# Mixture-of-experts stage: six second tiles of 64 places, with the high and the low parts of the tokens side by side in the stationary operand

## The chip, the cores and the metric

The kernel runs on one core of one Trainium2 chip. The metric is the device time of one execution in microseconds, as the median of several runs. The engines are called PE (TensorE; PEld are its weight loads), ACT (ScalarE), DVE (VectorE), POOL (GpSimd) and SP (SyncE, which issues transfers).

## The reference, cut to what matters

One layer of a hybrid model on 1024 tokens of width 1024: projections, sparse attention and a state-space mixer, an output projection, a layer norm, then a mixture of 16 experts with two experts per token, and a last layer norm. The change touches the experts alone:

```python
gates = ...            # top 2 of 4 experts in the best of 4 groups, times the group's probability
y = jnp.zeros_like(h)
for e in range(N_EXPERTS):                                  # 16
    hid = jax.nn.silu(h @ w_gate[e]) * (h @ w_up[e])        # 1024 -> 256
    y = y + gates[..., e:e + 1] * (hid @ w_down[e])         # 256 -> 1024
x = layer_norm(ALPHA * x + y, ln2_g, ln2_b)
```

All of it is fp32. The kernel keeps fp32's precision by splitting each operand of a product into a high part, which is its value in the reduced type that PE multiplies, and a low part, the remainder.

## The kernel before, in words

The stages up to the first layer norm are the same in both kernels. The router sorts the tokens into one list per expert (`lst`, 1152 places each, empty ones filled with indices that the indirect transfers skip). `order()` ranks the experts by how many tokens they have; ranks 0 to 3 are picked early, from the first blocks of tokens. An expert is worked on in tiles of 128 places of its list. `plan()` (L99) says which tiles are written out: ranks 0 and 1 have their first tile early, while the last two token blocks are still mixed, and their second tile in the main loop; ranks 2 to 7 have two tiles; ranks 8 to 15 have one. The order of the experts is `TURN` (L96): 0, 1, 2, 3, 8, 9, 4, 10, 11, 5, 12, 13, 6, 14, 15, 7. What an expert has over its written-out places (`CAPS`, L38: 256 places for ranks 0 to 7, 128 for the others) goes through a loop under `tc.If` at the end (L1282 ff.), which is skipped if no expert has more.

`expert_tile` (L892) does one tile:

1. `gather` (L885) fetches the tile's 128 rows of the normed tokens by an indirect transfer that POOL issues (`xg`).
2. PE transposes them in eight pieces (L898, tile `pt`), ACT casts each half to its high part `th` (helper `hi_act`, L123), DVE subtracts for the low part `tl` (helper `lo_dve`, L126).
3. PE multiplies with the gate and up weights (L909, tile `ag`, 512 columns: 256 of gate, 256 of up): eight pieces of the width, three products each (high by high, low by high, high by low), 24 matmuls.
4. ACT does SiLU on the gate half (L914), DVE multiplies by the up half (L915, `sg`).
5. PE transposes the 256 columns in two pieces (L918, `ph`), ACT and DVE split them again (`hh`, `hl`).
6. PE multiplies with the down weights (L934, tile `ad`, two halves of 512 columns, two pieces, three products: 12 matmuls). DVE multiplies the first half by the gate (L939), ACT the second (L937), into `yt`.
7. POOL issues the indirect scatter-add of `yt` into `yd` (L941).

The weights of an expert come in three pieces: gate and up for the first half of the width (key 0), for the second half (key 1), and down (key d), 1 MB each. `fetch` (L855) issues the transfers from SP into one of `NR` = 5 raw buffers `er`, in turn. `split_expert` (L867) makes the high part on ACT and the low part on DVE, in four quarters, into slots; 12 slots, in the tiles `eb`, `woh` and `wol`, hold two experts, so that an expert's piece goes where that of the expert two turns earlier was. When a piece is split, `more` issues the fetch that will reuse its raw buffer, five pieces further on. `yt` has three buffers, `xg` four, the others two; the gathers run three tiles ahead.

The order of instructions on each engine isn't written by hand: the program is given to a scheduler with a timeline of its own, which fixes for every engine one queue in which nothing overtakes. An instruction that waits in it holds up all that stand behind.

The main loop over the tiles begins at about 618 us of the profile; the scatter-add of the last tile is issued at 844.85.

Of the kernel before, what the change touches and what calls it, by code (L numbers as in the profile page):

```python
# [22 lines left out]
P = 128  # L23
# [13 lines left out]
SL = S + P  # L37
CAPS = ((0, 8, 256), (8, 16, 128))  # L38
XB = 4
# [59 lines left out]
def plan():  # L99
    return [(a, t) for a in TURN for t in ((P,) if a < NEARLY else (0, P) if a < 8 else (0,))]  # L100


# [7 lines left out]
def body(ctx, tc, I, out, dbg):  # L110
# [773 lines left out]

    def gather(ids, al):  # L885
        xg = al([P, D], F32, "xg")
        marks["gather"] = G.indirect_dma_start(out=xg, out_offset=None, in_=hd,
                                               in_offset=bass.IndirectOffsetOnAxis(ap=ids[:, 0:1], axis=0),
                                               bounds_check=S - 1, oob_is_err=False)
        return xg  # L890

    def expert_tile(W, ids, xg, al):  # L892
# [34 lines left out]
        for hf in range(2):  # L927
# [10 lines left out]
            else:  # L938
                V.tensor_scalar(yt[:, fs], ad_, gate, None, op0=OP.mult)  # L939
        yield  # L940
        st_ = G.indirect_dma_start(out=yd, out_offset=bass.IndirectOffsetOnAxis(ap=ids[:, 0:1], axis=0),  # L941
                                   in_=yt, in_offset=None, compute_op=OP.add,
                                   bounds_check=S - 1, oob_is_err=False)
        if "y" in W:
            tc.declare_no_dep(st_.ins, W["y"], reason="the two tiles of one expert hold distinct tokens")
        W["y"] = st_.ins
        yield

    with ExitStack() as ph:
# [253 lines left out]
        with (tc.manual_schedule(engines={getattr(mybir.EngineType, e) for e in MAN}) if MAN else ExitStack()):  # L1203
# [12 lines left out]
            for j in range(NG0):  # L1216
                ids = rp.tile([P, 2], I32, name="ids", bufs=XB + 2)
                SY.dma_start(ids, lst[bass.ds(EE[PLAN[j][0]] * SL + PLAN[j][1], P), :])
                early_q.append((ids, gather(ids, al0), PLAN[j][0]))
            with tc.issue_after(marks["gather"].ins) if NG0 else ExitStack():  # L1220
# [27 lines left out]
    def ids_for(r, t0):  # L1248
        ids = wk.tile([P, 2], I32, name="idt", bufs=len(PLAN) - NG0)
        SY.dma_start(ids, lst[bass.ds(rank(r) * SL + t0, P), :])  # L1250
        return ids, r

# [9 lines left out]
    for i in range(-AHEAD, len(PLAN)):  # L1262
        sp = []
        if NG0 <= i + AHEAD < len(PLAN):
            ids, r = lists.pop(0)
            q.append((ids, gather(ids, al1), r))
        if i >= 0:
# [6 lines left out]
        if i >= 0:  # L1274
            ids, xg, r = q.pop(0)
            t_ = expert_tile(WS[r], ids, xg, al1)
            emit((6, up(t_, HP)), *sp)
# [87 lines left out]
```

## Time and profile before

| | us |
|---|---|
| three runs, median | 889.72 |
| three runs, lowest and highest | 881.93, 892.22 |
| the profiled execution | 886.67 |
| its span | 885.0 |
| PE busy in the span | 784.3 (89%) |
| DVE, ACT, POOL busy | 655.7, 510.3, 240.1 |

The profile is that of one execution. The span goes from the first to the last instruction; the profiled execution's own time is 1.67 us longer. A matmul's end is modelled and overlaps the next one's start, so that the mean of single matmuls is longer than the step from one to the next; the chain of waits goes from start to start. A wait is put down to the releaser that came last.

### The profile page before, as it was taken

The numbers are of one execution on the slowest core, as the hardware profiler recorded it, in microseconds if no ns is written. First come the engines' busy times: TensorE is split into PE (matmuls) and PEld (weight loads), VectorE is DVE, ScalarE is ACT, GpSimd is POOL, SyncE is SP. The second block draws the span as 40 slices with busy tenths as digits, with TensorE's granted clock in tenths as the row PEclk, the third lists the DMA queues.
The fourth block names the chain that finished last, engine by engine and source line by source line (L and its number), as shares of the span: only waits on it lengthen the run. The fifth ranks groups of instructions, "written<-read, shape, count | busy, mean of one in ns | idle before, by whom it ended". The sixth has DMA issues, their size and how long they took to land. (4 is left out here: it accounts for less than half of the span.)

```text
span 885.0 us, 12823 instructions
## 1 busy us (share of the span) xinstructions
PE 784.3 (89%) x4084; PEld 647.0 (73%) x4085; DVE 655.7 (74%) x1619; ACT 510.3 (58%) x1083; POOL 240.1 (27%) x219
## 2 busy tenths in 40 slices
PE   6999789999997899899999999897899899999910
PEld 4798568887775678778888887775688688888700
DVE  3578988869578899778687676686586778887336
ACT  3467777892356677575464332263566767876333
POOL 3211000000377545170100111122433234332236
PEclk9999899999997999999999999899799999999965
DMA  8303122311335313884433323795699898987174
GB/s 245 102 26 96 38 71 81 116 55 60 110 113 186 117 60 111 279 281 163 119 120 120 113 103 120 258 371 156 148 345 316 238 307 270 325 269 231 26 214 192
DMA packets 90598, 147.57 MB, mean 167 GB/s; under 512 B 16645, under 2 KB 62869, under 8 KB 90522
## 3 DMA queue, kind: packets, MB, share of 16 engines
q1 hardware_dynamic: 83098, 129.87, 43.3%
q0 software_dynamic: 7424, 16.81, 8.2%
q8 instruction: 33, 0.54, 0.3%
q14 instruction: 43, 0.35, 0.1%
HBM read 109.78 MB, written 45.25 MB: 175 GB/s over the span
## 5 line engine op out<-in xcount | busy, mean ns | idle before, releaser
L231 PE MATMUL acc<-whl,xh 128*128 128x512 f32 (+1 forms) x384 | 121.4, 390 | 3.9 <-DVE rt L251 2.0
L231 PEld LDWEIGHTS acc<-whl,xh 128*128 128x128 f32 x384 | 72.5, 190 | 19.3 <-ACT whl L123 2.4
L252 POOL TENSOR_TENSOR r<-rt,rt 128x448 f32<-128x448 f32 (+1 forms) x16 | 22.9, 1429 | 196.4 <-DVE rt L251 179.8
L123 ACT ACTIVATE ph<-pt 128x512 fp32r<-128x512 f32 (+1 forms) x80 | 43.3, 551 | 56.4 <-PE pt L776 53.6
L231 PE MATMUL acc<-whl,xl 128*128 128x512 f32 (+1 forms) x192 | 75.7, 395 | 0.0
L909 PE MATMUL ag<-eb,th 128*128 128x512 f32 x192 | 68.7, 422 | 3.7 <-ACT th L123 3.7
L359 PE MATMUL acc<-xh,whl 128*128 128x512 f32 x192 | 64.0, 411 | 6.7 <-ACT u L123 6.7
L941 POOL DMA_INDIRECT yd<-yt,idt x21 | 40.4, 1922 | 103.7 <-ACT hh L123 31.8
L764 ACT ACTIVATE lt<-lt,mn 128x1024 f32<-128x1024 f32 (+7 forms) x64 | 49.3, 773 | 11.2 <-DVE mn L761 10.9
L126 DVE TENSOR_TENSOR plo<-pt,ph 128x512 fp32r<-128x512 f32 (+1 forms) x80 | 49.8, 630 | 6.4 <-ACT ph L123 5.9
L397 ACT ACTIVATE scra<-sc,mid 128x1024 bf16<-128x1024 f32 (+3 forms) x56 | 49.2, 879 | 4.2 <-DVE gef L427 1.7
L359 PEld LDWEIGHTS acc<-xh,whl 128*128 128x128 f32 x192 | 37.8, 199 | 15.4 <-ACT u L123 7.5
L1098 POOL DMA_INDIRECT lst<-pay,idx x16 | 18.3, 1146 | 113.3 <-DVE pay L1095 29.2
L123 ACT ACTIVATE eb<-er 128x512 fp32r<-128x512 f32 x64 | 38.1, 628 | 16.9 <-DMA er<-w_up 10.6
L879 DVE TENSOR_TENSOR eb<-er,eb 128x512 fp32r<-128x512 f32 x64 | 41.6, 687 | 8.2 <-ACT eb L123 4.7
L909 PEld LDWEIGHTS ag<-eb,th 128*128 128x128 f32 x192 | 38.4, 200 | 12.6 <-ACT th L123 4.5
L879 DVE TENSOR_TENSOR woh<-er,woh 128x512 fp32r<-128x512 f32 x64 | 41.7, 686 | 6.2 <-ACT woh L123 2.3
L879 DVE TENSOR_TENSOR wol<-er,wol 128x512 fp32r<-128x512 f32 x64 | 40.8, 683 | 7.2 <-ACT wol L123 4.3
L126 DVE TENSOR_TENSOR tl<-pt,th 128x512 fp32r<-128x512 f32 x48 | 32.3, 685 | 18.3 <-ACT th L123 18.2
L776 PE MATMUL pt<-ident,lt 128*128 128x128 f32 x288 | 44.7, 275 | 1.3 <-ACT lt L764 0.7
L123 ACT ACTIVATE woh<-er 128x512 fp32r<-128x512 f32 x64 | 37.9, 626 | 13.0 <-PE ac L1010 6.7
L1010 PE MATMUL ac<-woh,ai 128*128 128x512 f32 x128 | 43.7, 425 | 0.3 <-DVE xb L1014 0.3
(360 smaller groups left out, 2347.2 us busy)
## 6 DMA issues: line engine op xcount, KB each, us to landing
er<-w_gate SPq DMA_DIRECT2D x32, 512.0 KB
er<-w_up SPq DMA_DIRECT2D x32, 512.0 KB
er<-w_down SPq DMA_DIRECT2D x16, 1024.0 KB
xb<-x SPq DMA_DIRECT2D x16, 512.0 KB
raw<-w_in SPq DMA_DIRECT2D x8, 512.0 KB
qd<-qs SPq DMA_DIRECT2D x8, 512.0 KB
sd<-so SPq DMA_DIRECT2D x8, 512.0 KB
qb<-qd SPq DMA_DIRECT2D x8, 512.0 KB
```

The source lines that it names most:

```text
L123: A.activation(hi, src, AF.Copy)
L126: V.tensor_tensor(lo, src, f(hi), op=OP.subtract)
L231: T.matmul(acc[:, :n], l[:, b, k, :], r[:, k % 2, :n], start=i == 0, stop=i == 3 * KC - 1)
L252: G.tensor_tensor(dst, t1, t2, op=OP.add)
L359: T.matmul(acc, w[:, k, :], xx[:, 4 * hf:4 * hf + 4, k, :], start=i == 0, stop=i == 3 * KC - 1)
L397: A.activation(scra[:, :nk], sc[b], AF.Sign, bias=at, scale=-1.0, accum_out=dst)
L764: A.activation(lt[:, :nk], lt[:, :nk], AF.Exp, bias=mn[:, h:h + 1], scale=-1.0, accum_out=rs[:, h:h + 1])
L776: T.transpose(pt[:, c:c + P], L[b, 2 * p + j][:, kt * P:(kt + 1) * P], ident)
L879: e.tensor_tensor(lo[x], raw[x], f(hi[x]), op=OP.subtract)
L909: T.matmul(ag, l[:, k, :], r[:, k % 4, :], start=i == 0, stop=i == 3 * KC - 1)
L941: st_ = G.indirect_dma_start(out=yd, out_offset=bass.IndirectOffsetOnAxis(ap=ids[:, 0:1], axis=0), in_=yt, in_offset=None, compute_op=OP.a ...
L1010: T.matmul(ac, src[:, o + k % 4, :], w[:, k, fs], start=i == 0, stop=i == 3 * KC - 1)
```

## The change

`plan()` stays; a new function names the second tiles of ranks 2 to 7 as half tiles of 64 places (`HR`), and `CAPS` gives these ranks 192 places in all. For a half tile `half_tile` takes the place of `expert_tile`. Its operand `th` holds for each piece of the width 64 columns of high parts and then 64 columns of low parts of the same tokens. Each piece is multiplied with the high and then with the low part of the weights: two matmuls of 128x512 where there were three. Rows 0 to 63 of the result belong to the high parts, rows 64 to 127 to the low parts; ACT copies the lower rows over, DVE adds them to the upper ones. This is done for gate and up (into `yt`, which serves as the place for that sum too) and for both halves of the down product. The token's gate is multiplied in with the up part, behind the SiLU. The gather and the scatter-add name 64 places. The diff's core:

```diff
-CAPS = ((0, 8, 256), (8, 16, 128))
+CAPS = ((0, 2, 256), (2, 8, 192), (8, 16, 128))
+HR = P // 2
...
+def half(a, t):
+    return a >= NEARLY and t > 0
...
+    def half_tile(W, ids, xg, al):
+        th = al([P, KC, 2, HR], F32R, "th")
+        pt = psum([P, KC, HR], "pt", "pt")
+        for k in range(KC):
+            T.transpose(pt[:, k, :], xg[:HR, k * P:(k + 1) * P], ident[:HR, :HR])
+        hi_act(th[:, :, 0, :], pt)
+        lo_dve(th[:, :, 1, :], pt, th[:, :, 0, :])
+        yield
+        ag = psum([P, 512], "ag", "lg")
+        for k in range(KC):
+            for j, w in enumerate(W[k // 4]):
+                T.matmul(ag, th[:, k], w[:, k % 4, :], start=k + j == 0, stop=k + j == KC)
+            if k % 4 == 3:
+                yield
+        yt = al([P, D], F32, "yt")
+        sg = al([P, 256], F32, "sg")
+        A.activation(yt[:HR, :512], ag[HR:], AF.Copy)
+        V.tensor_tensor(yt[:HR, :512], ag[:HR], yt[:HR, :512], op=OP.add)
+        A.activation(sg[:HR], yt[:HR, :256], AF.Silu)
+        V.scalar_tensor_tensor(sg[:HR], yt[:HR, 256:512], f(ids[:HR, 1:2]), sg[:HR], op0=OP.mult, op1=OP.mult)
+        ph2 = psum([P, 2, HR], "ph2", "po")
+        for k in range(2):
+            T.transpose(ph2[:, k, :], sg[:HR, k * P:(k + 1) * P], ident[:HR, :HR])
+        hh = al([P, 2, 2, HR], F32R, "hh")
+        hi_act(hh[:, :, 0, :], ph2)
+        lo_dve(hh[:, :, 1, :], ph2, hh[:, :, 0, :])
+        yield
+        for hf in range(2):
+            fs = slice(hf * 512, (hf + 1) * 512)
+            ad_ = psum([P, 512], "ad", "sb" if hf else "sa")
+            for k in range(2):
+                for j, w in enumerate(W["d"]):
+                    T.matmul(ad_, hh[:, k], w[:, k, fs], start=k + j == 0, stop=k + j == 2)
+            A.activation(yt[:HR, fs], ad_[HR:], AF.Copy)
+            V.tensor_tensor(yt[:HR, fs], ad_[:HR], yt[:HR, fs], op=OP.add)
+        yield
+        add_rows(W, ids, yt, HR)
+        yield
...
-            t_ = expert_tile(WS[r], ids, xg, al1)
+            ids, xg, r, h = q.pop(0)
+            t_ = (half_tile if h else expert_tile)(WS[r], ids, xg, al1)
```

`gather` and `add_rows` (the scatter-add of `expert_tile`, now a function) take the number of places as an argument. Up to the expert stage the order of instructions is the same but for one more constant. In the stage the scheduler lays out everything anew. Two places:

The first place is on PE, from the end of rank 4's last down matmuls (`ad` of `woh`) on. Before, the rest of rank 10's gate-and-up matmuls follows (`ag` of `wol`), then transposes and matmuls of rank 11 (`ag` of `eb`); rank 12's use of its second gate-and-up piece comes 125 matmuls and 40 transposes after that end:

```order
L934 MATMUL ad<-woh,hl 128x512
L934 MATMUL ad<-woh,hh 128x512
L909 MATMUL ag<-wol,tl 128x512
L909 MATMUL ag<-wol,th 128x512 x2
...
L898 MATMUL pt<-ident,xg 128x128 x4
L909 MATMUL ag<-eb_6648,th 128x512
L909 MATMUL ag<-eb_6648,tl 128x512
```

Now (L989 and L968 are the half tile's down and gate-and-up matmuls, L947 and L922 those of whole tiles) the last three of rank 5's first tile follow, rank 5's half tile, and rank 10's down matmuls (`ad` of `wol`); behind these stand the transposes `ph` of rank 11 and the first twelve matmuls of rank 12:

```order
L989 MATMUL ad<-woh,hh 128x512 x8
L931 MATMUL ph_8334<-ident,sg 128x128 x2
L922 MATMUL ag<-wol,th 128x512
L922 MATMUL ag<-wol,tl 128x512
...
L968 MATMUL ag<-woh,th 128x512 x8
L968 MATMUL ag<-wol,th 128x512 x8
L911 MATMUL pt<-ident,xg 128x128 x4
L947 MATMUL ad<-wol,hh 128x512 x2
```

Down matmuls now stand further behind the gate-and-up matmuls of their tile, so that rank 12's second piece (`ag` of `eb_6651`) is used 43 matmuls and 13 transposes after rank 4's end.

The second place is on ACT, at the end of the stage. Before, the last instructions are those of rank 7's two tiles (the numbered `ph` are the transposed results, `yt` the evictions):

```order
L937 ACTIVATE yt<-ad,idt 128x512
L123 ACTIVATE hh<-ph_9308 128x256
L937 ACTIVATE yt<-ad,idt 128x512
L914 ACTIVATE sg<-ag 128x256
L123 ACTIVATE hh<-ph_9379 128x256
L937 ACTIVATE yt<-ad,idt 128x512
```

Now the copy of the half tile's gate-and-up result into `yt` (L973) stands behind the casts of rank 7's first tile (`ph_9244`), and its SiLU (L975) behind that tile's eviction:

```order
L950 ACTIVATE yt<-ad,idt 128x512
L128 ACTIVATE hh<-ph_9173 128x256
L950 ACTIVATE yt<-ad,idt 128x512
L128 ACTIVATE hh<-ph_9244 128x256
L973 ACTIVATE yt<-ag 64x512
L950 ACTIVATE yt<-ad,idt 128x512
L975 ACTIVATE sg<-yt 64x256
L128 ACTIVATE hh<-ph_9306 128x2x64
L990 ACTIVATE yt<-ad 64x512 x2
```

The half tile's gate-and-up matmuls themselves have moved forward, ahead of rank 14's down matmuls; the copy waits for the scatter-add of rank 14, whose `yt` buffer it takes.

## Rows read from the trace of the kernel before

**Rows 1.** The page's first part: busy us, share of the span, instructions

```profile
PE 784.3 (89%) x4084; PEld 647.0 (73%) x4085; DVE 655.7 (74%) x1619; ACT 510.3 (58%) x1083; POOL 240.1 (27%) x219
```

**Rows 2.** Stretches: us, busy PE, PEld, DVE, ACT, POOL; granted clock, DMA share, GB/s

```profile
650.00:690.00 40.00, 40.00 (x196) 32.66 (x195) 30.98 (x53) 29.16 (x54) 12.90 (x9) 1.00 0.99 316
690.00:710.00 20.00, 17.02 (x79) 13.40 (x79) 15.24 (x27) 12.50 (x25) 5.26 (x4) 0.98 0.74 229
710.00:810.00 100.00, 100.00 (x480) 81.28 (x479) 81.34 (x140) 73.78 (x141) 31.47 (x18) 0.99 0.96 300
810.00:846.00 36.00, 32.10 (x149) 25.17 (x147) 16.35 (x28) 14.22 (x28) 10.19 (x6) 1.00 0.32 54
```

**Rows 3.** The chain of waits: start, us, what

```profile
722.64 2.80 PE ad L934 x12
...
725.89 2.81 PE ag L909 x12
728.71 0.44 PE pt L898 x4
```

**Rows 4.** PE in order of time, ahead of the stage: start, us busy

```profile
590.27 0.97 PE L1028 MATMUL pr<-gbw,rT 128*128 128x20 f32 x8
```

**Rows 5.** Groups of ACT and DVE from 618 to 850: busy us, mean ns

```profile
L123 ACT ACTIVATE th<-pt 128x512 fp32r<-128x512 f32 x44 | 25.4, 595 | 16.4 <-PE pt L898 15.9
L126 DVE TENSOR_TENSOR tl<-pt,th 128x512 fp32r<-128x512 f32 x44 | 29.6, 685 | 17.5 <-ACT th L123 17.4
L939 DVE TENSOR_SCALAR yt<-ad,idt 128x512 f32<-128x512 f32 x21 | 15.6, 745 | 9.3 <-PE ad L934 9.1
L937 ACT ACTIVATE yt<-ad,idt 128x512 f32<-128x512 f32 x21 | 14.2, 677 | 20.0 <-PE ad L934 17.9 <-issue 2.1
L915 DVE TENSOR_TENSOR sg<-ag,sg 128x256 f32<-128x256 f32 x22 | 9.2, 419 | 14.0 <-ACT sg L914 13.8
L914 ACT ACTIVATE sg<-ag 128x256 f32<-128x256 f32 x22 | 8.3, 377 | 17.6 <-PE ag L909 17.6
```

**Rows 6.** One wait on ACT, PE behind it, the stretch after, the chain there

```profile
703.18 1.16 ACT L123 ACTIVATE wol<-er 128x512 fp32r<-128x512 f32 x2 [3.14 <-DMA er<-w_up]
708.04 0.49 PE L909 MATMUL ag<-eb,th 128*128 128x512 f32 x1 [2.98 <-ACT th L123]
708.00:712.50 4.50, 4.46 (x12) 3.43 (x13) 1.68 (x4) 0.75 (x2) 1.61 (x1) 0.62 0.74 194
709.04 4.37 PE ag L909 x12
```

**Rows 7.** One round of a raw buffer: down matmul, split, fetch, split, use

```profile
691.69 0.40 PE L934 MATMUL ad<-wol,hh 128*128 128x512 f32 x1
692.40 1.89 DVE L879 TENSOR_TENSOR wol<-er,wol 128x512 fp32r<-128x512 f32 x3
694.90 8.26 DMA er<-w_up
703.84 1.29 DVE L879 TENSOR_TENSOR wol<-er,wol 128x512 fp32r<-128x512 f32 x2 [2.35 <-ACT wol L123]
728.30 0.41 PE L909 MATMUL ag<-wol,th 128*128 128x512 f32 x1
```

**Rows 8.** The page's DMA queues: packets, MB, share of 16 engines

```profile
q0 software_dynamic: 7424, 16.81, 8.2%
```

**Rows 9.** Scatter-adds: count, median us to landing; rank 14's last matmul and issue

```profile
yd<-yt,idt POOLq DMA_INDIRECT x21, 9.6
822.91 0.40 PE L934 MATMUL ad<-wol,hh 128*128 128x512 f32 x1
824.59 1.90 POOL L941 DMA_INDIRECT yd<-yt,idt  x1 [6.61 <-ACT hh L123]
```

**Rows 10.** The stage's end: transposes of the last tile; chain at the last scatter-add

```profile
839.88 0.44 PE L918 MATMUL ph<-ident,sg 128*128 128x128 f32 x2 [1.27 <-DVE sg L915]
844.85 4.61 DMA yd<-yt,idt
```

More of the change, by code (lines that the diff above doesn't have):

```diff
@@ L883, in split_expert, with gather, add_rows @@
             yield
-    def gather(ids, al):
+    def gather(ids, al, n=P):
         xg = al([P, D], F32, "xg")
-        marks["gather"] = G.indirect_dma_start(out=xg, out_offset=None, in_=hd,
-                                               in_offset=bass.IndirectOffsetOnAxis(ap=ids[:, 0:1], axis=0),
+        marks["gather"] = G.indirect_dma_start(out=xg[:n], out_offset=None, in_=hd,
+                                               in_offset=bass.IndirectOffsetOnAxis(ap=ids[:n, 0:1], axis=0),
                                                bounds_check=S - 1, oob_is_err=False)
         return xg
+    def add_rows(W, ids, yt, n=P):
+        st_ = G.indirect_dma_start(out=yd, out_offset=bass.IndirectOffsetOnAxis(ap=ids[:n, 0:1], axis=0),
+                                   in_=yt[:n], in_offset=None, compute_op=OP.add,
+                                   bounds_check=S - 1, oob_is_err=False)
+        if "y" in W:
+            tc.declare_no_dep(st_.ins, W["y"], reason="the two tiles of one expert hold distinct tokens")
+        W["y"] = st_.ins
     def expert_tile(W, ids, xg, al):
@@ L940, in expert_tile @@
         yield
[L941 to L946, printed above, removed]
+        add_rows(W, ids, yt)
+        yield
[36 more added lines that the diff above has]
+        add_rows(W, ids, yt, HR)
         yield
@@ L1218, in body @@
                 SY.dma_start(ids, lst[bass.ds(EE[PLAN[j][0]] * SL + PLAN[j][1], P), :])
-                early_q.append((ids, gather(ids, al0), PLAN[j][0]))
+                early_q.append((ids, gather(ids, al0), PLAN[j][0], False))
             with tc.issue_after(marks["gather"].ins) if NG0 else ExitStack():
@@ L1250, in ids_for @@
         SY.dma_start(ids, lst[bass.ds(rank(r) * SL + t0, P), :])
-        return ids, r
+        return ids, r, half(r, t0)
     turn, last = [], {}
@@ L1264, in body @@
         if NG0 <= i + AHEAD < len(PLAN):
-            ids, r = lists.pop(0)
-            q.append((ids, gather(ids, al1), r))
+            ids, r, h = lists.pop(0)
+            q.append((ids, gather(ids, al1, HR if h else P), r, h))
         if i >= 0:
@@ L1274, in body @@
         if i >= 0:
-            ids, xg, r = q.pop(0)
-            t_ = expert_tile(WS[r], ids, xg, al1)
+            ids, xg, r, h = q.pop(0)
+            t_ = (half_tile if h else expert_tile)(WS[r], ids, xg, al1)
             emit((6, up(t_, HP)), *sp)
```

## The prediction, made before the changed kernel had run

> **What bounds the kernel now.** I read the page first, then the stretches, then the chain of waits, the rows of single engines, and last the order of instructions. The page has TensorE (PE) busy for 89% of 885.0 us [rows 1]; the change touches only the expert stage, from about 618 us on, so the stage has to be read alone. The stretches show PE busy for all of 650 to 690 and all of 710 to 810, with 20 us between in which 3 us are idle. VectorE (DVE) and ScalarE (ACT) are at 81% and 74% in the long stretch. The DMA engines are at 0.99 and 0.96, nearly as full as PE [rows 2]. The chain of waits in this stage is PE work, group behind group without a hole: 12 matmuls of 512 columns take 2.80 or 2.81 us, 0.234 us each; four transposes take 0.44 us, 0.109 each [rows 3]. So a matmul that goes here is worth 0.234 us as long as what feeds PE keeps up. After 846 us comes the final layer norm, which the change leaves alone.
>
> The sum is made against the profiled execution: 886.67 us, its span of 885.0 and 1.67 around it. The three runs have their median at 889.72, 3.05 higher, and lie between 881.93 and 892.22; a single execution of this kernel says nothing below half a per cent.
>
> **What is removed.** Six tiles (the second ones of ranks 2 to 7) go from 24 gate-and-up matmuls to 16 and from 12 down matmuls to 8: the stationary operand holds 64 tokens' high parts and the same tokens' low parts, so two products do the work of three (and one more, low by low, comes free). That is 6 x 12 = 72 matmuls x 0.234 = **16.8 us** off PE.
>
> The 8 + 2 transposes per tile remain, with 64 columns where there were 128. Bounds for 60 of them: nothing saved, or half of 0.109 each, 3.3 us. The nearest row is a run of eight small fp32 matmuls with 20 columns that are busy for 0.97 us, 0.12 each [rows 4]: so narrow, and no cheaper than the transposes of 128. I take **0** and keep 3.3 as the end.
>
> The matmul's price has a second reading. The loads of weights are 81.28 us busy in the same 100 us, 479 of them, 0.17 us each, with every load behind a matmul [rows 2]. The Trainium skill, Perfetto Trace Analysis, section Identifying the Most-Contended Engine, says that matmul busy time tells badly how close TensorE is to its limit, and that the share of LDWEIGHTS is the fair measure. By it PE would have a fifth to spare, and 72 removed loads would be worth 12.2 us, not 16.8. The chain's rows, which go from start to start, speak for 0.234.
>
> **What is added.** ACT gets three 64x512 copies out of PSUM for one 128x512 eviction and one of two 128x512 casts; DVE gets three 64x512 additions likewise. Taking a 64-row instruction as dear as a 128-row one: ACT +2 x 0.677 - 0.595 = 0.76 us a tile, DVE +2 x 0.745 - 0.685 = 0.81 [rows 5]; at half price both fall. Six tiles: at most 5 us each, beside engines that have 19 and 26 us free in 100 [rows 2]. I cost it at nothing where PE work covers it; where the cover is gone is the last tile, below.
>
> The gathers and scatter-adds name 64 places instead of 128. That moves no fewer bytes: the software queue moved 16.81 MB [rows 8], and 2 x 1024 tokens x 4096 bytes, gathered once and added once, are 16.78 MB, so empty places cost nothing already. DMA keeps its load.
>
> **What is moved, first: the weight ring.** The scheduler lays the whole stage out anew. In the copy before, 28 to 43 us of PE work stand between the last down matmul of an expert and the first use of the second gate-and-up piece of the expert four turns later; now 11.5 us (rank 4 to rank 12, the piece shown: 43 matmuls and 13 transposes), 13.4, 13.6, 13.9, 15.3, and seven between 17 and 33. This distance matters since five raw buffers go round: the down weights two turns on can be split only when the slot is free, the split frees a raw buffer, and that buffer takes the fetch of the very piece named. The trace has one such loop complete: the down matmuls end at 692.09, the split at 694.29, the fetch issued at 694.90 lands 8.26 us later, the first quarter is split at about 704.5: **12.4 us**; PE first used it at 728.30, 24 us after [rows 7]. That cover is what goes. The DMA share was 0.74 in that stretch and is 0.96 in the long one [rows 2]; scaled so, the landing takes 10.7 us and the loop 14.9. The low end is 12.4; the high end is another megabyte queued ahead, 12.4 + 8.26 = 20.7. At 14.9 the loops of 11.5, 13.4, 13.6 and 13.9 fall short by 3.4 + 1.5 + 1.3 + 1.0 = 7.2 us. Such a wait stands in ACT's queue before the casts of the next tile, as the one wait of this kind in the trace shows: ACT waited 3.14 us for w_up, the cast behind it came late, PE idled 2.98 us, and the granted clock was 0.62 in the 4.5 us after, so that 12 matmuls of the chain took 4.37 us, not 2.81 [rows 6]. So one stall of 3 us costs 1.6 more at the lower clock: 8.8 us in all. The old stall (2.98 + 1.6 = 4.6) is of the same kind and is counted back: net **+4.2 us**.
>
> A second way to the same size: shares times stretches [rows 2] are 39.6 + 14.8 + 96 = 150.4 us of full DMA work in 160. PE's share of that stretch would fall to 160 - 5 x 2.8 - 4.6 = 141.4. If the DMA engines can't go above what they move, 9.0 us of the PE gain come back there, and -16.8 - 4.6 + 9.0 and the tail below make about the same sum.
>
> **What is moved, second: the tail.** yt has three buffers. A tile used to take one at its down matmuls; the half tile takes one for its gate-and-up result, a step earlier. For the last tile (rank 7, second) that buffer is rank 14's, whose scatter-add must have landed. The order puts only 24 matmuls and 4 transposes (6.05 us) between rank 14's last down matmul and the transposes that wait for this. In the trace rank 14's down matmuls end at 823.31 and its scatter-add is issued at 824.59, 1.28 later; landing took 4.61 us for the last one of all and 9.6 in the median [rows 9, 10]. DMA is at 0.32 there [rows 2], so I take 5.5, near the low end. Copy, addition, SiLU and product follow: 0.68 + 0.75 + 0.38 + 0.42. That is 9.0 us against 6.05, an idle of 2.95 where PE idled 1.27 before [rows 10]. So +1.7; eight matmuls at the lower clock (12 took 1.6 more, so 8 take 1.1 more); and at the end a copy stands ahead of the addition, +0.7. Net **+3.5 us**; with a landing of 9.6 it is 7.6.
>
> **Sum.** -16.8 + 4.2 + 3.5 = -9.1, so 886.67 - 9.1 = 877.6; call it **878**, since the median of the runs lies above the profiled one.
>
> **Rivals.** (a) The ring holds: fetches go out earlier as slots come free earlier, the loop stays at 12.4, nothing but 0.9 us is short. For it: the 24 us of cover in [rows 7]. Against it: most of that cover is no longer in the order. Then -16.8 - 4.6 + 0.9 + 3.5 = -17.0: 869.7, and 865 if the transposes halve and the tail lands fast.
> (b) Slower: the ring becomes the bound. The place is the split of the down weights and the fetch behind it. It decides from a loop of about 16.3 us on, where shortages and lower clock together eat 18 us. At 17 us the five short loops lack 3.1 + 1.7 + 5.5 + 3.4 + 3.6 = 17.3 and four of them lose 1.6 more at the lower clock: 23.7 - 16.8 - 4.6 + 3.5 = +5.8, **892**; at 18 about 900. For it: the DMA share near 1 and a fetch that already takes 8.26 us at 0.74. Against: a late piece also delays what would fill the queue.
> (c) The loads of weights price the matmul: the sum with 12.2 in place of 16.8 gives 882.2. The chain's rows speak against it.
> (d) The change does not do what it says: an expert of rank 2 to 7 with over 192 tokens would go through the slow loop at the end, some 30 us for its unhidden weights, gather and tile. Run on the reference's own inputs the router gives 202, 182, 181, 171, 153, 136 as the largest counts; the largest is in rank 0, which keeps 256 places. Hardly possible.
>
> **How the numbers follow.** Forecast 0.48, (a) 0.25, (b) 0.18, (c) 0.06, (d) 0.03. One per cent, about what a measurement of this kernel can tell from no change, is 8.9 us, so the forecast lies on that bound: half of it counts as faster. Faster by over 1%: 0.24 + 0.25 = 0.49. Slower by over 1%: 0.14 of (b) and (d), 0.17. Within: 0.34. The range that holds the time 8 times in 10 goes from 865 ((a) with its extras) to 893 ((b) at its threshold and somewhat over); the forecast's own is 870 to 886.
>
> **What would show it.** Right: 72 fewer matmuls in the stage and its PE busy time down by about 17 us; ACT rows that wait for er<-w_up or w_down more often than now, PE idle behind them, and the granted clock dropped after; a PE idle of 3 us or more before the last transposes, ended by DVE's product, with the last scatter-add of rank 14 behind it; nothing changed before 618 us and after the last scatter-add. Wrong: PE without holes from 650 to the end (then (a)); PE idle of 15 us and more (then (b)); the same pace of 0.234 lost in the half tiles, which would show in the chain as groups of 8 that take more than 1.9 us; or ACT or DVE over 95% busy, which I count out.

## The result, and the profile after

The changed kernel takes 900.4 us in the median of four runs (897.83 to 902.57), the kernel before 890.14 in the same comparison: a ratio of 1.0147 with a 95% interval from 1.0108 to 1.0185. It is slower by 1.5%, where 878 us and a range up to 893 were forecast. The profiled execution took 902.57 us, its span is 900.9.

The page's first part and the software queue [rows 1, 8]:

```profile
PE 779.6 (87%) x4012; PEld 638.8 (71%) x4013; DVE 657.7 (73%) x1625; ACT 509.3 (57%) x1089; POOL 234.9 (26%) x220
...
q0 software_dynamic: 6656, 16.81, 8.0%
```

72 matmuls are gone, and still PE is busy for only 4.7 us less, where 16.8 were to go. ACT and DVE have the work that they had, the gathers and scatter-adds their bytes. The stretches [rows 2]:

```profile
650.00:690.00 40.00, 36.24 (x169) 28.30 (x169) 27.99 (x48) 25.05 (x49) 11.17 (x8) 0.95 0.79 257
690.00:710.00 20.00, 19.73 (x91) 15.16 (x89) 12.87 (x23) 11.62 (x25) 5.21 (x4) 0.92 0.71 216
710.00:810.00 100.00, 88.68 (x404) 70.11 (x405) 75.22 (x131) 65.92 (x128) 24.73 (x19) 0.93 0.89 277
810.00:846.00 36.00, 32.36 (x141) 24.59 (x139) 26.07 (x47) 22.64 (x45) 7.12 (x5) 0.95 0.62 182
```

In the long stretch PE did 404 instructions in place of 480, was idle for 11 us and had a granted clock of 0.93 in place of 0.99. The DMA engines, too, do less in it (0.89 for 0.96): neither is full, so something waits. The difference of the spans, 15.9 us, splits in three. The main loop's first transposes start at 623.99 instead of 621.52 (2.5 us; nothing was changed ahead of them, and in the profiles below their start varies between 614.7 and 624.3). From there to the end of the last down matmul the stage takes 233.5 us instead of 222.3 (+11.2; below "the stage" is this length). From that end to the end of the span it is 43.4 us instead of 41.1 (+2.3).

What ACT waited for in the stage, first before, then after (engine, what it did next, what it waited for; us in total, times, longest):

```profile
ACT wol L123 <- DMA er<-w_up: 3.6, 2, 3.1
ACT woh L123 <- DMA er<-w_up: 3.6, 2, 2.0
...
ACT eb L123 <- DMA er<-w_up: 1.9, 1, 1.9
```

```profile
ACT eb L128 <- DMA er<-w_up: 14.6, 8, 5.3
...
ACT woh L128 <- DMA er<-w_up: 9.8, 5, 2.5
...
ACT wol L128 <- DMA er<-w_up: 1.0, 1, 1.0
```

25.4 us of waiting for weights, not 9.1. PE's waits from 640 us on rise from 4.8 to 22.2 us. Of ACT's 25.4 us, 17.8 (nine of the 14 waits) are for first gate-and-up pieces. How one comes from the other is seen at the first place. SP's issues (start, length), ACT, PE, and stretches of 5 us [rows 6, 7]:

```profile
665.12 2.80 SPq L869 DMA_DIRECT2D er<-w_up  x1
687.78 0.37 SPq L869 DMA_DIRECT2D er<-w_gate  x1
688.36 0.37 SPq L869 DMA_DIRECT2D er<-w_up  x1
688.92 0.37 SPq L867 DMA_DIRECT2D er<-w_down  x1
689.48 0.37 SPq L869 DMA_DIRECT2D er<-w_gate  x1
690.03 0.61 SPq L869 DMA_DIRECT2D er<-w_up  x1
709.27 0.37 SPq L869 DMA_DIRECT2D er<-w_gate  x1
```

```profile
681.59 2.20 ACT L128 ACTIVATE eb<-er 128x512 fp32r<-128x512 f32 x4 [5.35 <-DMA er<-w_up]
683.70 1.13 ACT L128 ACTIVATE woh<-er 128x512 fp32r<-128x512 f32 x2
684.85 0.59 ACT L990 ACTIVATE yt<-ad 64x512 f32<-64x512 f32 x1
685.35 1.14 ACT L128 ACTIVATE woh<-er 128x512 fp32r<-128x512 f32 x2
686.39 0.58 ACT L990 ACTIVATE yt<-ad 64x512 f32<-64x512 f32 x1
686.99 0.38 ACT L128 ACTIVATE hh<-ph 128x256 fp32r<-128x256 f32 x1
...
695.52 2.19 ACT L128 ACTIVATE eb<-er 128x512 fp32r<-128x512 f32 x4
...
702.31 2.20 ACT L128 ACTIVATE woh<-er 128x512 fp32r<-128x512 f32 x4 [1.59 <-DMA er<-w_up]
```

```profile
680.37 2.03 PE L989 MATMUL ad<-woh,hh 128*128 128x512 f32 x8
...
687.43 0.79 PE L947 MATMUL ad<-wol,hh 128*128 128x512 f32 x1 [3.48 <-ACT hh L128]
```

```profile
675.00:680.00 5.00, 5.00 (x23) 4.03 (x22) 2.77 (x6) 1.25 (x3) 0.00 (x0) 1.00 0.67 205
680.00:685.00 5.00, 3.95 (x23) 3.07 (x21) 2.74 (x5) 3.38 (x7) 0.77 (x1) 1.00 0.07 23
685.00:690.00 5.00, 2.29 (x5) 1.58 (x6) 4.88 (x9) 3.92 (x8) 2.00 (x2) 0.62 0.36 97
690.00:695.00 5.00, 5.00 (x21) 4.07 (x20) 1.91 (x4) 1.59 (x4) 0.61 (x2) 0.69 1.06 363
```

Read it like this. A fetch issued at 665.12, the last of several close together, lands at 681.6, 16 us later ([rows 7]: 8.26). Behind this wait in ACT's queue stand the split of a down piece (`woh` at 683.70, whose slot rank 2's last down matmuls at 680.37 had just left) and the cast `hh` that PE needs: PE idles 3.48 us, and the granted clock of the 5 us is 0.62, mostly the lower of its levels (1.2 GHz). Meanwhile SP issues nothing for 22.7 us, since its next fetch goes into the raw buffer that this down piece leaves; the DMA engines fall to 0.07. When the piece is split, five transfers go out in 2.3 us and the DMA engines are full (1.06). The first piece of them is split at 695.52 without a wait, 7.2 us after its second half was issued; for the last of the five, issued at 690.03, ACT waits until 702.31. The three longest gaps between fetches from 645 us on are 22.7, 19.2 and 23.6 us (from 734.01 to 757.61); before the longest was 13.2.

The order of ACT shows how the scheduler brought it about. `er4`, the down piece of rank 8 (`TURN`'s fifth), is split behind three pieces that were fetched after it; `er3` in the fourth row is the one that came late. The pieces in `er0` and `er1` are split ahead of it, so their buffers are free while the fetch into `er4`'s buffer holds the queue:

```
581 L128 ACTIVATE woh_4061<-er0_6644 128x512 x4
582 L128 ACTIVATE hh_7697<-ph2_7694 128x2x64
583 L128 ACTIVATE wol_4062<-er1_6645 128x512 x4
584 L128 ACTIVATE eb0_6649<-er3_6647 128x512 x4
585 L128 ACTIVATE woh_4061<-er4_6648 128x512 x2
```

Two counts from the orders go with the experiments. The lag is the PE work between a tile's last gate-and-up and its first down matmul, as a mean over the main loop's 22 tiles (0.234 us a matmul, 0.109 a transpose): 8.8 us before, 18.2 after. Late splits are the pairs in which a piece's last quarter is split on ACT behind that of a piece fetched after it: 15 before, 24 after.

### The profile page after: what moved, and what is told of

The parts are those of the page before. It is cut to its first block, busy times and chain, and to the rows that moved or that the text cites. A ratio compares the mean times of both kernels' runs of the same rounds, so it can differ in the third digit from the quotient of the medians.

```text
span 900.9 us, 12656 instructions
## 1 busy us (share of the span) xinstructions
PE 779.6 (87%) x4012; PEld 638.8 (71%) x4013; DVE 657.7 (73%) x1625; ACT 509.3 (57%) x1089; POOL 234.9 (26%) x220
## 3 DMA queue, kind: packets, MB, share of 16 engines
q0 software_dynamic: 6656, 16.81, 8.0%
## 5 line engine op out<-in xcount | busy, mean ns | idle before, releaser
L898 POOL DMA_INDIRECT yd<-yt,idt x21 | 37.6, 1793 | 106.5 <-DVE yt L991 33.5
L922 PE MATMUL ag<-eb,th 128*128 128x512 f32 x144 | 52.6, 433 | 2.3 <-DVE yt L974 1.6
L884 DVE TENSOR_TENSOR woh<-er,woh 128x512 fp32r<-128x512 f32 x64 | 41.4, 687 | 16.9 <-ACT woh L128 13.5
L884 DVE TENSOR_TENSOR eb<-er,eb 128x512 fp32r<-128x512 f32 x64 | 40.9, 686 | 17.0 <-ACT eb L128 15.9
L128 ACT ACTIVATE eb<-er 128x512 fp32r<-128x512 f32 x64 | 36.1, 624 | 27.6 <-DMA er<-w_up 24.3
L788 PE MATMUL po<-ph,vhl 128*128 128x256 f32 x144 | 42.5, 310 | 1.8 <-DVE yo L709 1.0
L788 PE MATMUL po<-plo,vhl 128*128 128x256 f32 x144 | 40.6, 303 | 1.6 <-DVE plo L131 1.6
```

The source lines that it names most:

```text
L128: A.activation(hi, src, AF.Copy)
L788: T.matmul(po, vhl[:, kt, :], x[:, i * 256:i * 256 + 256], start=kt == 0 and x is ph_, stop=kt == b and x is pl_)
L884: e.tensor_tensor(lo[x], raw[x], f(hi[x]), op=OP.subtract)
L922: T.matmul(ag, l[:, k, :], r[:, k % 4, :], start=i == 0, stop=i == 3 * KC - 1)
```

## The experiments

Comparisons are by the ratio to the kernel before, which ran in each group (its medians: 886.2 to 890.1); a difference in us between two groups is rough by some us. Stage, waits and orders are those of one profiled execution each, and the scheduler lays out every kernel anew, so that an edit can move more than the thing it names.

| run | us | ratio to before, 95% | stage | ACT waits for er | lag | late splits |
|---|---|---|---|---|---|---|
| before | 890.1 | 1 | 222.3 | 9.1 | 8.8 | 15 |
| changed | 900.4 | 1.015 (1.011 to 1.019) | 233.5 | 25.4 | 18.2 | 24 |
| own_sum | 880.0 | 0.990 (0.986 to 0.994) | 210.0 | 14.0 | 13.4 | 14 |
| six_raw | 910.7 | 1.025 (1.021 to 1.029) | 242.9 | 26.9 | 18.1 | 32 |
| padded | 910.2 | 1.024 (1.020 to 1.029) | 244.9 | 41.8 | 18.9 | 23 |
| before_early_yt | 885.6 | 0.997 (0.995 to 0.999) | 222.9 | 17.9 | 11.9 | 16 |
| ring_order | 894.3 | 1.008 (1.005 to 1.011) | 227.7 | 13.5 | 18.4 | 16 |
| own_sum_ring_order | 877.9 | 0.988 (0.983 to 0.993) | 207.6 | 12.5 | 14.8 | 9 |
| before_ring_order | 884.0 | 0.994 (0.991 to 0.997) | 217.4 | 0.7 | 8.2 | 13 |
| no_low_rows | 882.8 | 0.992 (0.989 to 0.996) | 214.0 | 17.3 | 11.2 | 20 |
| four_yt | 895.1 | 1.010 (1.007 to 1.013) | 228.6 | 32.2 | 17.7 | 20 |
| own_sum_padded | 903.4 | 1.020 (1.015 to 1.025) | 240.4 | 13.4 | 10.9 | 19 |
| own_sum_ring_order_four_yt | 872.7 | 0.984 (0.980 to 0.989) | 208.8 | 12.4 | 14.8 | 9 |
| before_six_raw | 881.6 | 0.993 (0.991 to 0.996) | 216.5 | 0 | 8.2 | 15 |
| own_sum_six_raw | 876.9 | 0.988 (0.983 to 0.992) | 208.4 | 12.9 | 14.5 | 23 |
| own_sum_ring_order_six_raw | 872.7 | 0.986 (0.980 to 0.992) | 205.2 | 3.6 | 14.6 | 9 |
| own_sum_ring_order_six_raw_2 | 873.4 | 0.983 (0.979 to 0.987) | 205.3 | 1.2 | 14.6 | 9 |
| before_ring_order_six_raw | 882.0 | 0.992 (0.988 to 0.995) | 217.1 | 0 | 8.2 | 13 |
| six_raw_two_queues | 892.6 | 1.005 (1.003 to 1.007) | 221.1 | 0 | 17.1 | 32 |
| own_sum_six_raw_two_queues | 875.4 | 0.986 (0.983 to 0.989) | 211.3 | 7.3 | 14.6 | 32 |

### The early yt

```diff
-        yt = al([P, D], F32, "yt")
+        ys = f(al([P, KC, P], F32R, "tl")).rearrange("p k c -> p (k c)")
...
-        A.activation(yt[:HR, :512], ag[HR:], AF.Copy)
-        V.tensor_tensor(yt[:HR, :512], ag[:HR], yt[:HR, :512], op=OP.add)
+        A.activation(ys[:HR, :512], ag[HR:], AF.Copy)
+        V.tensor_tensor(ys[:HR, :512], ag[:HR], ys[:HR, :512], op=OP.add)
...
         lo_dve(hh[:, :, 1, :], ph2, hh[:, :, 0, :])
         yield
+        yt = al([P, D], F32, "yt")
```

> The changed kernel, but the half tile keeps the sum of its gate-and-up rows in a buffer of tl, which a half tile does not use, and takes yt only at its down matmuls, as a whole tile does. In the order of PE the mean distance from a tile's last gate-and-up matmul to its first down matmul is 13.4 us of matmuls (8.8 before, 18.2 in the changed kernel), and the distance from the end of an expert's down matmuls to the first use of the second gate-and-up piece four turns on is 20 us or more everywhere (11.5 in the changed kernel). Theory (the early yt lets the down matmuls slip, their slot and raw buffer come free late, the fetch is late, ACT stands waiting for er<-w_up and PE idles at a lower clock): ACT's waits for er fall from 25 us to about 10, PE idles fall from 27 us to 10 or 12, and the time falls to 876 to 886. Rival 1 (PE without the 72 matmuls outruns what the DMA engines bring, whatever the order): 895 to 902, with the same waits in other places. Rival 2 (the longer chain of the half tile, four steps between ACT and DVE, costs it): no change beyond the tail, 894 to 900.

Measured 880.0, 20 us below the changed kernel, with the same number of instructions on PE, DVE, ACT and POOL. Rival 1 falls, as the same fetches now fit into a stage that is 23.5 us shorter, and rival 2, as the longer chain is still there. Two gaps of 17.4 and 18.1 us between fetches remain from 645 us on, and cost PE little. ACT's waits in its profile, and the largest of PE's, which sum up to 6.5 us from 640 us on (22.2 in the changed kernel):

```profile
ACT woh L128 <- DMA er<-w_up: 7.2, 2, 4.2
...
ACT wol L128 <- DMA er<-w_up: 3.7, 2, 2.5
...
ACT eb L128 <- DMA er<-w_up: 3.1, 3, 2.1
```

```profile
PE ad L947 <- ACT hh L128: 4.5, 2, 3.7
```

The early buffer alone, in the kernel before, where SiLU's result takes its place and no copy or addition is added:

```diff
+        yt = al([P, D], F32, "yt") if early else None
+        sg = yt[:, :256] if early else al([P, 256], F32, "sg")
```

> The kernel before, with one thing of the change: the second tiles of ranks 2 to 7 take their yt buffer behind the gate-and-up matmuls and keep SiLU's result in it (sg is its first 256 columns). No matmul, copy or addition differs. The down matmuls move from 8.8 to 11.9 us behind in the mean, and the distance for the loop of a raw buffer falls from 28 to 43 us to 23 to 43. Theory (it is the loop of the raw buffers that counts, with a price of 15 to 20 us): still covered, so no more than a few us: 888 to 895. Rival 5 (waiting for the scatter-add of three tiles earlier is itself the cost, some 2 us for each of six tiles on ACT): 898 to 905.

It costs nothing (885.6): the lag rises by 3 us only. So it takes both, the early buffer and the half tile; which part of the half tile was not separated. Is it the wait for that buffer on the chip, then? One more buffer shortens this wait:

```diff
-    wkb = {"xg": XB, "yt": 3}
+    wkb = {"xg": XB, "yt": 4}
```

> The changed kernel with four yt buffers in the place of three and nothing else: the half tile still takes its buffer early, but that of four tiles back. The scatter-adds wait for one another (one is issued when the one before has landed, in the changed kernel every 9 to 19 us), so with three buffers the half tile's copy can stand in ACT's queue until the scatter-add of three tiles back has landed. The scheduler's order keeps its late down matmuls (17.7 us behind in the mean), pieces split behind a later one fall from 24 to 20. Second theory (the order and the fetch queue cost, the buffer only led the scheduler to it): 890 to 899. Third theory (the waits for landed scatter-adds on the chip are the cost themselves): 878 to 886, as with the sum in its own buffer.

At 895.1 most of the loss is still there, so the third theory falls. The changed kernel's trace says the same: from 640 us on ACT waits for a landed scatter-add once, 1.9 us in the tail. The late order stays (lag 17.7).

### The ring

With one more raw buffer:

```diff
-NR = 5
+NR = 6
```

> The changed kernel with six raw buffers in the place of five (NR = 6); the order of PE keeps its late down matmuls (mean distance 18.1 us, shortest loop 10.5). Theory that the ring of raw buffers is what turns late down matmuls into waits: each fetch is issued one piece earlier, so a piece has some 4 us more to land; ACT's waits for er fall to less than half of 25 us and the time falls to 882 to 890. Rival 1 (the DMA engines are the bound): 897 to 902, the waits stay. Rival 3 (late down matmuls stall PE and the splits by the slots alone, not by the raw buffers): 896 to 902, with ACT waiting for down matmuls rather than for er.

It got slower, 910.7, against every expectation. For the forecast's loop of five buffers this was the wrong sign. Late splits rise to 32, and four gaps of 17 to 22 us between fetches each end with that of a down piece. The new sequence puts an expert's down piece behind the next expert's gate-and-up pieces (`SEQ` takes the place of `3 * n + i` in `raw_of`, `more1` and the loop over splits):

```diff
+    SEQ = [(n, i) for n in range(2) for i in range(3)]
+    for n in range(2, NE + 1):
+        SEQ += [(n, 0), (n, 1)] if n < NE else []
+        SEQ += [(n - 1, 2)] if n > 2 else []
```

> The changed kernel with one thing else: the sequence in which the pieces go round the five raw buffers. The down piece of an expert comes behind the two gate-and-up pieces of the next expert and not ahead of them. yt is taken early as in the changed kernel, and the order of PE keeps its late down matmuls (18.4 us behind in the mean, shortest loop 10.9 us). In the order of ACT the number of times that a piece is split behind a piece that was fetched after it falls from 24 to 16 (15 in the kernel before, 14 with the sum in its own buffer, 32 with six raw buffers). Second theory (the fetches stand in one queue on SP; a down piece that is split late holds up the fetch into its buffer and all fetches behind it, and when it is split they go out in one burst): the gaps of 20 us between fetches shrink, ACT's waits for er fall from 25 us to 10 to 15, and the time falls to 880 to 892. Forecast's mechanism (the distance from an expert's down matmuls to the second piece four turns on): the distances are the same, so 895 to 905. Rival 3 (late down matmuls cost through the slots alone): 896 to 903.

894.3, 0.7% below the changed kernel with the same lag: the fetch queue is part of it, and a smaller one than expected. The same on the other two kernels:

> Both edits together: the half tile's sum in its own buffer and the down piece behind the next expert's gate-and-up pieces in the ring. Pieces split behind a later one: 9 (14 with the first edit alone). Second theory: the gaps between fetches shrink further and the waits of ACT for er (14 us with the first edit alone) go below 8: 868 to 877. If the first edit already removed what the fetch queue costs: 877 to 883. If the order that the scheduler finds now (down matmuls 14.8 us behind in the mean, 13.4 with the first edit alone) counts more: 883 to 890.

> The kernel before with the new sequence of the ring alone. There the down matmuls stand 8.2 us behind, and pieces are split behind a later one 13 times, now mostly a gate-and-up piece behind a down piece, against 15. Second theory: little to gain, 884 to 893. If the new sequence is worth something by itself, whatever the order: 872 to 882.

877.9 can't be told from the 880.0 without it. The kernel before gains half a per cent, its waits for er vanish (0.7 us). Was it the fetch queue, or are late down matmuls dear as such? In the last group the down pieces are fetched from ACT's queue, so that they can't stand ahead of the others:

```diff
-                SY.dma_start(raw, src)
+                (SY if n < 4 else A).dma_start(raw, src)
```

> The changed kernel with six raw buffers, of which a gate-and-up piece uses four and a down piece two in turn, as in the earlier run with six; the fetches of the down pieces from the fifth expert on are issued by ACT and no longer by SP, so that they cannot hold up the others (ACT loads twelve indices of experts for it). yt is taken early; down matmuls 17.1 us behind in the mean (18.1 in the run with six), pieces split behind a later one 32, as there. If the single queue of fetches is what turned late splits into waits: gaps of 20 us between fetches of gate-and-up pieces vanish, and the time falls from 910 to 880 to 892. If the late down matmuls cost as such, by the order on ACT and PE: 900 to 912. If issuing on ACT costs much by itself, over 912.

892.6, 18 us below the same kernel with one queue, with the order hardly better: the stage falls from 242.9 to 221.1 us, PE's waits from 30.9 to 11.6. What ACT waited for in the run with one queue, and then with two:

```profile
ACT woh L128 <- DMA er<-w_up: 16.8, 4, 5.8
...
ACT eb L128 <- DMA er<-w_up: 7.4, 4, 2.9
ACT woh L128 <- PE ad L989: 7.1, 2, 4.5
```

```profile
ACT wol L128 <- PE ad L989: 11.5, 2, 5.9
ACT woh L128 <- PE ad L989: 10.9, 2, 5.9
```

Every wait for a fetch is gone. What is left are ACT's waits for late down matmuls, whose slots its splits need; that they make the rest of the loss is likely and not shown. Its control, and six buffers on the other kernels:

> The same two queues with the sum in its own buffer (down matmuls 14.6 us behind, pieces split behind a later one 32 as in the run beside it). If the single queue of fetches still costs there: 868 to 875, against 876.9 with one queue. If it does not: 875 to 880. If issuing on ACT costs by itself: over 880.

> The kernel with the sum in its own buffer, with six raw buffers and the old sequence of pieces. Down matmuls 14.5 us behind in the mean (13.4 with five), pieces split behind a later one 23 (14 with five). Second theory: the sixth buffer is eaten up by the later splits of the down pieces, 880 to 892, no better than the 880 with five. If more buffers simply let fetches go earlier: 870 to 877.

> The kernel before with six raw buffers. The order of PE is as before (down matmuls 8.2 us behind in the mean), pieces split behind a later one 15, as with five. If a sixth buffer costs by itself (a megabyte more in flight ahead of gathers and scatter-adds): 893 or more. Second theory (the order in which pieces are split against the order in which they are fetched decides): 878 to 887, since the waits for late fetches, 9 us on ACT, shrink.

Both single-queue kernels with a normal order gain or hold with a sixth buffer (881.6 and 876.9), so it does not cost by itself. own_sum_six_raw went against the second theory: 23 late splits and no loss. The number of late splits alone does not decide, nor does the lag alone (10.9 in own_sum_padded below, which is slow). The slow runs without added matmuls all have a lag of 17 us or more, the fast ones 15 or less; why that is the border is not shown. On the kernel with a normal order two queues bring nothing that can be told (875.4).

The Trainium skill, DMA: Bandwidth & Descriptors, section Issuing engines are not separate DMA queues, says that starting transfers from several engines saves only the time that their sequencers take to start them. For bandwidth no run here speaks against it; for a queue whose head waits the two runs do, 910.7 against 892.6.

### What the removed matmuls are worth, and the best version

Half tiles brought back to 24 and 12 matmuls (the first line is that of gate and up):

```diff
-            for j, w in enumerate(W[k // 4]):
+            for j, w in enumerate((W[k // 4][0],) + W[k // 4]):
...
-                for j, w in enumerate(W["d"]):
+                for j, w in enumerate((W["d"][0],) + W["d"]):
```

> The changed kernel with the half tile's matmuls brought back to 24 and 12: each product with the high part of the weights is done twice, so the time alone can be read (its sums count that part twice). PE has the work of the kernel before, everything else is as changed, yt is taken early, and the down matmuls stand 18.9 us behind in the mean. Theory (the order costs, through late fetches): the stalls stay nearly the size they have in the changed kernel since they are counted in us of DMA and not of PE, while PE has 16.8 us more work, part of which covers the waits: 905 to 915. Rival 1 (the fetches bound the stage): the time of the changed kernel, 897 to 903, since the added matmuls fill idle time. Rival 4 (the loss lies in the half tile's own matmuls, at a slower pace): 917 or more.

> The kernel with the sum in its own buffer, its half tiles brought back to 24 and 12 matmuls as in the padded run (products with the high part done twice, so its sums count that part twice). Down matmuls 10.9 us behind in the mean, pieces split behind a later one 19. The price of a matmul: at 0.234 us each, 72 of them, 16.8 us more than without them, 893 to 900; if they fall into time in which PE waits anyway (the fetches are the bound), 880 to 888; with 0.17 us each, 12.2 us: 890 to 893.

The added matmuls did not all fall into idle time: 910.2 is 10 us above the changed kernel, and 903.4 is 23 above own_sum, more than the 16.8 that they take. So the fetches' rate is not the bound. But own_sum_padded does as many matmuls as the kernel before and is 2.0% slower, 17 us. In its stage PE idles for 14.4 us (before 6.0) and is busy for 226.0 us with the same 1012 instructions (216.3), at a granted clock of 0.95 (0.97). Is this the longer chain at the gate-and-up result?

```diff
-        A.activation(yt[:HR, :512], ag[HR:], AF.Copy)
-        V.tensor_tensor(yt[:HR, :512], ag[:HR], yt[:HR, :512], op=OP.add)
-        A.activation(sg[:HR], yt[:HR, :256], AF.Silu)
+        A.activation(sg[:HR], ag[:HR, :256], AF.Silu)
```

> The changed kernel, the half tile without the copy and the addition of its lower rows at the gate-and-up result: SiLU and the product read the upper rows from PSUM as a whole tile does, so the part of the sum that belongs to the tokens' low parts is left out there; yt is taken at the down matmuls. The chain between gate-and-up and down matmuls has two steps less on ACT and DVE. Down matmuls 11.2 us behind in the mean, pieces split behind a later one 20. Rival 2 (the longer chain and the extra copies and additions cost): better than the kernel with the sum in its own buffer, 866 to 875. Second theory (the fetch queue decides, 20 lies between 14 and 24): 880 to 890, no better than that kernel.

882.8, no better than own_sum, although a copy and an addition are gone from each of the six chains. Rival 2 falls in the form in which it was stated; what makes PE wait more in own_sum_padded stays open.

With the ring repaired on both sides:

> The sum in its own buffer, the new sequence of the ring, and six raw buffers; down matmuls 14.6 us behind in the mean, pieces split behind a later one 9, both as with five. Second theory: with the order kept, one more buffer can only help: 870 to 878, ACT's waits for er (12 us) go below 5. If a sixth buffer costs by itself (a megabyte more in flight ahead of gathers and scatter-adds), which would be why the changed kernel lost 10 us by it: 880 to 888.

> The sum in its own buffer, the new sequence and six raw buffers, now with every piece fetched. Pieces split behind a later one 9. Second theory: 870 to 876, ACT's waits for er below 5 us, the fastest so far. If a sixth buffer costs by itself: 880 or more.

> The kernel before with the new sequence and six raw buffers: 36 matmuls in every tile, down matmuls 8.2 us behind. With five buffers the new sequence alone left almost no wait for er, so no change is expected from the sixth: 880 to 886. If the 72 matmuls are worth their 16.8 us once the ring is repaired on both sides, this kernel stands 14 to 18 us above the run before it in this group; if the half tile's longer chain takes part of it back, 6 to 12.

> The sum in its own buffer, the new sequence of the ring, and four yt buffers; the order of PE is the same to the row as with three, ACT differs in one place. Third theory (waiting for landed scatter-adds still costs): 871 to 875. If the waits for yt are no longer on the path: 876 to 880, no change that can be measured.

In the first of these (872.7) one gate-and-up piece of rank 8 was never fetched, and its sums use what the buffer held; with every piece the time is 873.4. The kernel before with the same ring takes 882.0. There the half tiles bring 8.6 us, and 11.8 in the stage (217.1 to 205.3), not 16.8. The stages of this pair, before's first:

```profile
624.04:841.12 217.08, 214.16 (x1012) 172.39 (x1012) 164.44 (x278) 147.73 (x277) 67.37 (x47) 0.98 0.83 253
```

```profile
622.56:827.83 205.27, 200.84 (x940) 156.97 (x940) 162.34 (x283) 145.89 (x283) 75.04 (x46) 0.98 0.87 265
```

Of the 5.0 us that are missing, 1.5 are idle time of PE, and 3.5 lie in its busy time, which falls by 13.3 us. The two versions at 873 (sum in its own buffer, new sequence, and a fourth yt or a sixth raw buffer with every piece fetched) beat the kernel before by 1.6 and 1.7% and the changed one by 3%.

## Why the prediction was wrong

**Removed: right.** 72 matmuls are gone and the half tile's own go at the pace forecast. Two groups of eight follow one another by 1.95 and 1.87 us, 0.24 each, here in own_sum_ring_order, where no wait lies between:

```profile
816.29 2.11 PE L973 MATMUL ag<-woh,th 128*128 128x512 f32 x8
818.24 2.03 PE L973 MATMUL ag<-wol,th 128*128 128x512 f32 x8
820.11 0.63 PE L952 MATMUL ad<-woh,hh 128*128 128x512 f32 x2
```

The stage's gain of 11.8 with repaired rings lies near rival (c)'s 12.2 by chance: these rows leave no room for a cheaper matmul.

**Transposes: taken at nothing, and they cost a little.** In a row the narrow ones take 0.063 us each (the median step), not 0.109. But the matmul ahead of such a group takes 0.32 us to the next start, and three transposes 0.32, so that the four take 0.64 us where the forecast's prices give 0.56 for wide ones (also own_sum_ring_order):

```profile
809.08 0.39 PE L927 MATMUL ag<-wol,th 128*128 128x512 f32 x1
809.40 0.40 PE L966 MATMUL pt<-ident,xg 64*128 64x64 f32 x3
809.72 0.50 PE L927 MATMUL ag<-wol,tl 128*128 128x512 f32 x1
```

In the pair above, the steps from start to start into, within and out of transposes add up to some 2.4 us more with the half tiles: most of the 3.5 us of busy time that were not won.

**Added work and DMA load: right as sums** (DVE +2.0 us, ACT -1.0, 16.81 MB). The second way to the DMA bound, with its 9.0 us, failed: the share fell to 0.89.

**The ring: the step that failed.** Its place and its chain of causes are what the trace shows: late down matmuls, late split, late fetch, ACT's wait, PE's idle, lower clock. The loop's length came out as forecast, by luck. Rank 2's down matmuls end at about 682.2, the fetch they release goes out at 687.78, and its first quarter is split at 697.1, 14.9 us later:

```profile
696.43 2.48 DVE L884 TENSOR_TENSOR eb<-er,eb 128x512 fp32r<-128x512 f32 x4
```

The forecast had 2.8 us from the matmuls to the fetch and 10.7 for the landing. Here it is 5.6, since the split stood behind ACT's wait, and at most 7.2, with the DMA engines at 0.07 ahead of it.

What failed is who pays. "+4.2 us" took each short loop as one piece that comes a few us late, and found four such pieces, all second gate-and-up pieces. But a fetch that can't go holds up every fetch behind it on SP, though their buffers are free, and then all go out together. The last piece of such a group is a first gate-and-up piece, which is in none of the forecast's loops, and such pieces have 17.8 of the 25.4 us that ACT waits. The piece at 681.59, which cost PE the first 3.48 us, is one of them. The four short loops themselves have 4.7 us of ACT's waits (rank 12's 1.96 and rank 7's 2.78, which the profile puts down to SP), where 7.2 were forecast.

The term was 7.2 + 1.6 = 8.8 us of idle time and lower clock, less 4.6 for the old stall. Against that net 4.2 stand 11.2 + 16.8 = 28.0 us by which the stage, the idle time before the last transposes included, is longer than before's less the removed matmuls. The stages, before's first:

```profile
621.52:843.85 222.33, 216.33 (x1012) 173.86 (x1012) 163.66 (x278) 146.49 (x277) 72.29 (x47) 0.97 0.82 247
```

```profile
623.99:857.51 233.52, 210.11 (x940) 162.99 (x940) 164.44 (x283) 145.41 (x283) 64.22 (x46) 0.93 0.77 233
```

Idle time of PE makes up 17.4 of the 28.0 (23.4 less 6.0). The other 10.6 are busy time: PE is busy for 6.2 us less, not for 16.8. The forecast counted the lower clock once; in the trace it falls to its lower level (1.2 GHz) in four stretches behind waits, before in one (beside one at the stage's start in both). PE is busy at that level for 25.5 us of the stage, before for 11.8, and a matmul takes 0.43 us there instead of 0.234. That makes an estimate of 6 us; the remaining 4 are steps at the full clock, for the most part at transposes. What the queue's part is was measured with six buffers only: of the 34.5 us between the stages of six_raw and own_sum_six_raw (242.9, 208.4) two queues take back 21.8.

**The tail: right in size by luck, and wrong in scope.** Rank 14's scatter-add is issued at 845.06 and the copy that needs its buffer starts at 851.46, 6.4 us later (forecast 5.5):

```profile
851.46 0.60 ACT L973 ACTIVATE yt<-ag 64x512 f32<-64x512 f32 x1 [1.93 <-DMA yd<-yt,idt]
```

```profile
854.32 0.31 PE L979 MATMUL ph<-ident,sg 64*128 64x64 f32 x2 [1.68 <-DVE sg L976]
855.38 2.13 PE L989 MATMUL ad<-wol,hh 128*128 128x512 f32 x8 [0.75 <-DVE hh L131]
```

PE idles 2.4 us there, 1.2 more than before (+1.7 forecast); the eight matmuls run at the full clock (+1.1 forecast, 0 measured); and the end behind the last matmul is 2.3 us longer (+0.7 forecast). The sum is the forecast's 3.5, its terms are not. The end grows since the last scatter-add goes out 3.6 us behind the last down matmul, before 1.0: on POOL it stands behind that of rank 7's first tile, which goes out only at 859.23:

```profile
859.23 1.55 POOL L898 DMA_INDIRECT yd<-yt,idt  x1 [5.50 <-DVE yt L991]
861.09 1.41 POOL L898 DMA_INDIRECT yd<-yt,idt  x1 [0.30 <-issue]
```

And the prediction looked at the early yt in the last tile alone. The section on the change saw that down matmuls "now stand further behind the gate-and-up matmuls of their tile", and the prediction did not ask why. own_sum shows that the same early buffer, in all six tiles, was a good part of it (the lag falls from 18.2 to 13.4, with 8.8 before), and moving it took 20 us off.

**Chances.** Rival (b) had 0.18. It named the place and, at a loop of 18 us, the time of 900, but that number is luck too: no loop of 18 us was read, and the pieces that wait are others. Its argument against, that a late piece also delays what would fill the queue, holds for the first fetches after a gap (7.2 us at most) and not for the last of the five (12.3 us to ACT's split).

## What to carry to other kernels

A buffer is to be taken where it is first needed for good: taking it a step earlier changed no work, and cost 20 us in the half tiles by the order that it led the scheduler to, though nothing in the kernel before. On a queue in which nothing overtakes, price a late release by all that stands behind it and by the burst that follows, and compare the order in which buffers come free with the order in which they are refilled. When a change to a part off the bound moves an order, ask what moved it before pricing what follows.

## What was not expected of the hardware

A sixth raw buffer made one kernel 10 us slower and another 7 us faster; in the slower one a second queue took 18 us off. A fetch issued as the last of several took 16 us to land, twice, with ACT waiting for it (665.12 to 681.59, 719.87 to 736.04), against 8.26 in [rows 7]. And 72 matmuls were worth 23 us where they brought waits with them (own_sum_padded against own_sum), 10 in padded against the changed kernel, and 8.6 in the cleanest pair. Narrower transposes saved nothing: what they win in a row is lost at the group's two ends.
